# Four array tiles for the second token half of the chunk products, gates behind the last pair, a merged Nyquist product and a later norm, in an fp32 three-layer kernel

## The chip, the cores and the metric

One core of one Trainium2 chip. The metric is the device time of one execution in microseconds (us), as the median of three runs. The profile is that of one execution of its own, taken by the hardware profiler.

## What is computed

The input is 512 tokens of 1024 features, in fp32. A first block (feed-forward, token mixer, feed-forward, norm), an "even" layer (Fourier mixing beside attention) and an "odd" layer (gated linear recurrence) with a last norm follow each other. What the change touches of it:

```python
def first_block(x, ...):
    x = x + 0.5 * swiglu(rms_norm(x, ffn1_norm), ...)
    x = x + token_mixer(rms_norm(x, mix_norm), ...)
    x = x + 0.5 * swiglu(rms_norm(x, ffn2_norm), ...)
    return rms_norm(x, final_norm)

# token_mixer: p = h @ w_in; a gated convolution (y_a), and per head of 64
def step(S, inp):                      # wkv7, 512 tokens one after the other
    r_t, w_t, k_t, v_t, a_t, b_t = inp
    sa = einsum("bhvk,bhk->bhv", S, a_t)
    S = S * w_t + sa[..., None] * b_t + v_t[..., None] * k_t
    return S, einsum("bhvk,bhk->bhv", S, r_t)
y_b = (groupnorm(y) + bonus) * g @ w_out_b
return (sigmoid(g_a) * y_a + sigmoid(g_b) * y_b) @ w_o

# even layer: h = rms_norm_2(x, norm_g), f_in = 4 groups of 256 features
fmix = fftn(fg, axes=(1, 3), norm="ortho").real
fmix = einsum('bsgc,gce->bsge', fmix, fourier_w)
```

## The kernel before

Activations lie feature-major as tiles of 128 features by 512 tokens. TensorE has a fast fp32 form (fp32r) that keeps only a part of the digits, so every large product is written as three (`mm3`): a tile is split into a high half and the rest (`split`: `h`/`l`, weights `wh`/`wl`, scaled inputs `xh`/`xl`), and h·h, h·l and l·h are added up in PSUM. Such a matmul is `128*128 128x512 f32` in the rows. Weights come in groups of 128x1024 (`group`): `raw` is loaded, `wh` is cast from it on ACT or DVE, and `wl` is formed on DVE or, for many later weights, was written to DRAM during the first feed-forward (`low`) and is loaded again.

Nothing is issued where it is written. Class `Rec` records every operation; `schedule` then plays the program on a cost model (`_cost`, with buffers and PSUM banks counted) and picks the next instruction of each engine, mostly by its place in the program plus `rec.bias`; `choose` prefers, within limits, a matmul of the array mode in use. `emit` fixes the order that comes out. So the place of a call in the code is a priority, and a price in `_cost` can move work. All operations carry one line, L555 (L557 in the changed kernel).

The stages on the time axis: first feed-forward to about 400 us, mixer to about 740, second feed-forward to about 1140, even layer to about 1475, odd layer and last norm to the end.

In the mixer the 512 steps of the recurrence are done in 8 chunks of 64 tokens, for two heads at a time (a "pair", four of them). `pair(j)` makes the scaled keys, queries and so on; `pair_out(j)` does the chunks: `batch` forms their products, `inverse64` inverts 64x64 triangular matrices from 16x16 inverses in two levels (`p1 = b·TT`, copied to `x1`; `p2 = x1·T`, added to `T`), `pd = T·R` and `pq = ak·R` apply the inverse, `pm` makes the chunk's transition, and a chain over the chunks follows. These products are plain fp32 with operands of 64 partitions, and TensorE then works as four tiles of 64x64 (row half by column half). A product whose operand lies in partitions 0 to 63 uses the upper row half, and where it writes in PSUM says which column half. In `p1`, `p2`, `pd` and `pq` the chunk of half `c` is read from half `c` and written to half `c`, so that two of the four tiles work:

```python
            p1 = self.W((128, 8, 64))
            for m in range(8):
                for c in range(2):
                    k = slice(64 * c, 64 * c + 64)
                    PE.matmul(p1[k, m], b[k, m], TT[k, m], start=True, stop=True)
```

The other chunk products (`xy`, `pm`) use all four. The products of 64x64 stand in the rows as `64*64 64x64` or, with 128 columns, `64*64 64x128`; one such fp32 product leaves two records in the trace. `W` and `P` take one of 8 PSUM banks.

Around the chunk work, `conv`, `out_a`, `gate` and `gates` do the rest of the mixer with large matmuls. At its end, the last pair's `yc` is transposed, `yo` is formed from it on DVE and POOL, split into `h` and `l`, and used by `w_out_b`; the results `gt` go through POOL and a split into `w_o`.

In `_even`, two sums of squares of x (`sumsq`: squares on ACT, additions on DVE for the first and on POOL for the second) are folded over the partitions by matmuls with a matrix of ones (`fold`, in the rows `h,rones` and `l,rones`), and give `rs1` and `rs`; matmuls of the Fourier weights `e_f` start on the unnormed `xs` meanwhile. Then, for each of four groups, a first DFT (`d1h`, `d1l`), sums and differences `s`, `d` over the token halves, and three products over the other axis (`seq`), the third for one column only, the Nyquist one: `pn = seq(c2, 0)`, 12 matmuls of 256 columns, of which row 0 is used.

Of the kernel before, what the change touches and what calls it, by code (L numbers as in the profile page):

```python
# [71 lines left out]
_COFF["mI"] = _COFF["i64"] + 64  # L72
_COFF["mST"] = _COFF["mI"] + 64
_COFF["m16"] = _COFF["mST"] + 64
_COFF["e16"] = _COFF["m16"] + 64
_COFF["eps"] = _COFF["e16"] + 128
_COFF["reset"] = _COFF["eps"] + 4
_NC = _COFF["reset"] + 512
# [2 lines left out]
def _const_block():  # L81
    c = np.zeros((128, _NC), np.float64)
    p = np.arange(128)[:, None]
    q = np.arange(128)[None, :]
    same = (p // 64) == (q // 64)
    m = {
        "ident": p == q,
        "ones": np.ones((128, 128)),
        "bones": same,
    }  # L90
    for n in _CST:
        c[:, _COFF[n]:_COFF[n] + 128] = m[n]
# [4 lines left out]
    c[:, _COFF["m16"]:_COFF["m16"] + 64] = (w // 32 == p % 64 // 32) & (w % 32 < 16) & (p % 32 >= 16)  # L97
    c[:, _COFF["e16"]:_COFF["e16"] + 128] = np.repeat(np.eye(16).reshape(2, 128), 64, 0)
# [499 lines left out]
def _cost(o, outs, ins):  # L598
# [4 lines left out]
    if o.eng == "tensor":  # L603
        if o.fn == "matmul":
            m = _elems(ins[0])
            k = int(ins[0].shape[0])
            up = lambda i: 32 if i <= 32 else 64 if i <= 64 else 128
            o.mode = up(k), up(m)
            one = "float32r" in str(ins[0].dtype)
            c = n / 2.4 + 13.5 if one else max(n, m) / 0.6 + 10.0  # L610
            o.load = n / (2.4 if one else 0.6) * o.mode[0] * o.mode[1] / 16384.0
            if not one and m <= 64 and k <= 64:
                c = 31.0 if n <= 64 else 105.0
        else:
            o.mode = 128, 128
            c = 109.0
            o.load = 50.0
        return c, 0.0
# [29 lines left out]
class Net:  # L648
# [278 lines left out]
    def _mixer(self):  # L927
# [82 lines left out]
        conv(1)  # L1010
        conv(2)
        self.pair_out(*p.pop(0))
        conv(3)
        p[3] = pair(3)
        out_a(0)
        self.pair_out(*p.pop(1))
        out_a(1)
        out_a(2)
        self.pair_out(*p.pop(2))
        out_a(3)  # L1020
        gates(0, 4)
        self.pair_out(*p.pop(3))
        gates(4, 8)
        ms = []
        for h in range(4):
            w = self.group("w_out_b", h)
# [214 lines left out]
    def inverse64(self, ab, TT):  # L1241

        nc = self.nc
        V, A, PE = nc.vector, nc.scalar, nc.tensor
        f = lambda t: t.rearrange("p m i -> p (m i)")
        a16 = self.T(shape=(128, 8, 64), p="a16")
        nc.tt(a16, ab, self.c("m16", 64).unsqueeze(1).to_broadcast([128, 8, 64]), ALU.mult)
        for lvl in range(2):

            b = ab if lvl else a16  # L1250
            T = self.T(shape=(128, 8, 64), p="TN")
            V.transpose(out=f(T), in_=f(TT))
            p1 = self.W((128, 8, 64))
            for m in range(8):
                for c in range(2):
                    k = slice(64 * c, 64 * c + 64)
                    PE.matmul(p1[k, m], b[k, m], TT[k, m], start=True, stop=True)
            x1 = self.T(shape=(128, 8, 64), p="XT")
            A.copy(x1, p1)
            p2 = self.W((128, 8, 64))  # L1260
            for m in range(8):
                for c in range(2):
                    k = slice(64 * c, 64 * c + 64)
                    PE.matmul(p2[k, m], x1[k, m], T[k, m], start=True, stop=True)
            if lvl:
                for h in (0, 64):
                    V.tensor_tensor(T[h + 32:h + 64, :, 0:32], T[h + 32:h + 64, :, 0:32], p2[h + 32:h + 64, :, 0:32], ALU.add)
            else:
                V.tensor_tensor(T, T, p2, ALU.add)
                TT = self.T(shape=(128, 8, 64), p="TT")  # L1270
                V.transpose(out=f(TT), in_=f(T))
        return T

    def batch(self, AR, BK, BH, dF, vT, ab, TT):
# [10 lines left out]
        for tp in range(2):  # L1285

            xy = [self.W((128, 6, 64)) for _ in range(2)]
            for tt in range(2):
                for i in range(2):
                    for hh, cc in q4:  # L1290
                        PE.matmul(xy[hh][sl(cc), 2 * i + tt], BK[tp][sl(hh), tt, i, sl(cc)], AR[tp][sl(hh), tt, 1, sl(cc)],
                                  start=True, stop=True)
                for hh, cc in q4:
                    PE.matmul(xy[hh][sl(cc), 4 + tt], AR[tp][sl(hh), tt, 0, sl(cc)], BK[tp][sl(hh), tt, 1, sl(cc)],
                              start=True, stop=True)
            t = self.T(p="ak")[:, 0:256].rearrange("p (q s) -> p q s", q=4)
            for hh in range(2):
                V.tensor_tensor(RR[tp][hh].rearrange("p i t s -> p (i t) s")[:, :, 0:64], xy[hh][:, 0:4], mI, ALU.mult)
                V.tensor_tensor(t[:, 2 * hh:2 * hh + 2], xy[hh][:, 4:6], mST, ALU.mult)
            ak.append(t)  # L1300

        for tp in range(2):
# [8 lines left out]
            A.copy(t[:, 0], pa)  # L1311
# [4 lines left out]
        for tp in range(2):  # L1316
            pd = self.W((128, 4, 128))
            for hh in range(2):
                for tt in range(2):
                    q = 2 * hh + tt  # L1320
                    for cc in range(2):
                        PE.matmul(pd[sl(cc), q], T[sl(cc), 4 * tp + q], RR[tp][hh][sl(cc), 0, tt], start=True, stop=True)
            for hh in range(2):
                A.copy(RR[tp][hh][:, 0], pd[:, 2 * hh:2 * hh + 2])
        for tp in range(2):
            pq = self.W((128, 4, 128))
            for hh in range(2):
                for tt in range(2):
                    q = 2 * hh + tt
                    for cc in range(2):  # L1330
                        PE.matmul(pq[sl(cc), q], ak[tp][sl(cc), q], RR[tp][hh][sl(cc), 0, tt], start=True, stop=True)
            for hh in range(2):
                V.tensor_tensor(RR[tp][hh][:, 1], RR[tp][hh][:, 1], pq[:, 2 * hh:2 * hh + 2], ALU.add)
# [4 lines left out]
        for tp in range(2):  # L1338
# [3 lines left out]
            for tt in range(2):  # L1342
                for hh, cc in q4:
                    R = RR[tp][hh]
                    PE.matmul(pm[cc][sl(hh), tt, 0:128], aT[tp][sl(cc), 0, tt, sl(hh)], R[sl(cc), 0, tt], start=True, stop=True)
                for hh, cc in q4:
                    R = RR[tp][hh]
                    PE.matmul(pm[cc][sl(hh), tt, 128:192], R[sl(cc), 1, tt, 64:128], vT[sl(cc), 2 * tp + tt, sl(hh)],
                              start=True, stop=True)
            Rh = aT[tp][:, 1]  # L1350
            for cc in range(2):
                V.tensor_tensor(cc4(MT)[:, cc], pm[cc][:, :, 64:128], dv[:, cc, 2 * tp:2 * tp + 2], ALU.add)
                A.copy(cc4(N)[:, cc], pm[cc][:, :, 128:192])
# [9 lines left out]
    def _even(self):  # L1363
# [37 lines left out]
        for gp in range(2):  # L1401
# [10 lines left out]
        fo = []  # L1412
        for g in range(4):
            fs = []
            for m in range(2):
# [18 lines left out]
            V.tensor_tensor(s, pp[0], b, ALU.add)  # L1434
            V.tensor_tensor(d, pp[0], b, ALU.subtract)
            sd = (self.split(s, (128, 2, 256)), self.split(d, (128, 2, 256)))

            def seq(col, tr):
                ps = self.P((128, 2, 256))
                for e in range(2):  # L1440
                    h, l = sd[e]
# [410 lines left out]
```

## Time and profile before

| | |
|---|---|
| median of three runs | 1857.87 us (1857.47 to 1860.03) |
| the profiled execution's own time | 1858.05 us |
| its span, first to last instruction | 1856.3 us |
| TensorE busy | 1835.8 us, 99% |
| VectorE (DVE) busy | 1266.8 us, 68% |
| ScalarE (ACT) busy | 854.5 us, 46% |
| GpSimd (POOL) busy | 230.5 us, 12% |
| mean granted clock of TensorE | 0.997 of full |

The profiled execution lies 0.18 us above the median. The span and 1.75 us around it make its time.

### The profile page before, as it was taken

What the parts mean: (1) busy time and instruction counts of PE and PEld (TensorE: products, weight loads), DVE (VectorE), ACT (ScalarE), POOL (GpSimd) and SP (SyncE); (2) the same over time, 40 slices, a digit from 0 to 9 for tenths busy, and PEclk for the clock granted to TensorE, in tenths of its full rate; (3) what the DMA queues carried; (4) which work ended last, traced back from release to release, by engine and by line L of the source; (5) the groups of instructions that cost most, each with busy time, mean ns of one, the idle gap of its engine ahead of it and who ended that gap; (6) DMA issues with size and microseconds to landing.
All of it is one profiled execution on the core that took longest, in us unless ns stands there. A gap on an engine that the chain in (4) does not pass through costs nothing.

```text
span 1856.3 us, 26407 instructions
## 1 busy us (share of the span) xinstructions
PE 1835.8 (99%) x10344; PEld 1540.4 (83%) x10344; DVE 1266.8 (68%) x1966; ACT 854.5 (46%) x1188; POOL 230.5 (12%) x182
## 2 busy tenths in 40 slices
PE   9999999999999999999999999999999999999997
PEld 7888888888888886888878887888999888888887
DVE  7766775579767424476567668854478966899773
ACT  6333433465243332344344246422255645897771
POOL 0100101223202003211011015110000010000002
PEclk9999999999999999999999999999999999999999
DMA  7898895436534344578888874222212125466543
GB/s 270 285 311 283 299 318 173 142 128 172 189 120 139 131 154 157 176 260 291 271 273 306 283 239 146 81 69 79 89 50 72 54 102 188 169 204 210 193 170 103
DMA packets 120398, 341.10 MB, mean 184 GB/s; under 512 B 33873, under 2 KB 36177, under 8 KB 120273
## 3 DMA queue, kind: packets, MB, share of 16 engines
q1 hardware_dynamic: 120272, 339.41, 54.6%
q8 instruction: 81, 1.33, 0.3%
q14 instruction: 45, 0.36, 0.1%
HBM read 277.76 MB, written 61.60 MB: 183 GB/s over the span
## 4 chain that ended last, share of the span: by engine, by line
PE 53%; DMA 6%; DVE 5%; ACT 1%; issue 1%; POOL 1%; SPq 0%; POOLq 0%; DVEq 0%; ACTq 0%
PE pm L555 51%; DMA raw<-o_in 3%; PE pw L555 2%; DVE wl L555 2%; DMA low<-wl 2%; ACT wh L555 1%; DMA raw<-ffn_d 1%; DVE t L555 0%; DVE l L555 0%; DMA wl<-low 0%; POOL acc L555 0%; DVE x L555 0%; DVE xl L555 0%; DVE acc L555 0%; DVE s L555 0%
## 5 line engine op out<-in xcount | busy, mean ns | idle before, releaser
L555 ACT CAST wh<-raw 128x1024 fp32r<-128x1024 f32 (+1 forms) x331 | 343.8, 1042 | 670.6 <-PE pm L555 285.2
L555 PE MATMUL pm<-xh,wl 128*128 128x512 f32 x1488 | 580.6, 390 | 1.3 <-DVE wl L555 1.1
L555 PE MATMUL pm<-xh,wh 128*128 128x512 f32 x1488 | 581.3, 391 | 0.3 <-ACT wh L555 0.3
L555 PE MATMUL pm<-xl,wh 128*128 128x512 f32 x1488 | 580.6, 390 | 0.9 <-DVE xl L555 0.9
L555 DVE TENSOR_TENSOR wl<-raw,wh 128x1024 fp32r<-128x1024 f32 (+1 forms) x302 | 383.1, 1271 | 194.9 <-DMA low<-wl 86.7
L555 PEld LDWEIGHTS pm<-xh,wl 128*128 128x128 f32 x1488 | 279.4, 188 | 60.9 <-DVE wl L555 3.9
L555 PEld LDWEIGHTS pm<-xh,wh 128*128 128x128 f32 x1488 | 279.4, 188 | 58.7 <-ACT wh L555 0.7
L555 PEld LDWEIGHTS pm<-xl,wh 128*128 128x128 f32 x1488 | 279.4, 188 | 58.6 <-DVE xl L555 1.3
L555 PE MATMUL pm<-h,wl 128*128 128x512 f32 (+1 forms) x832 | 317.8, 382 | 2.1 <-DMA wl<-low 2.1
L555 PE MATMUL pm<-h,wh 128*128 128x512 f32 (+1 forms) x832 | 316.8, 383 | 1.8 <-DVE yo L555 0.9
L555 PE MATMUL pm<-l,wh 128*128 128x512 f32 (+1 forms) x832 | 317.5, 382 | 0.0
L555 POOL TENSOR_TENSOR t<-t,t 128x512 f32<-128x512 f32 x60 | 90.3, 1507 | 915.3 <-DVE t L555 693.7
L555 PEld LDWEIGHTS pm<-h,wl 128*128 128x128 f32 x832 | 156.8, 189 | 32.3 <-DMA wl<-low 2.6
L555 PEld LDWEIGHTS pm<-h,wh 128*128 128x128 f32 x832 | 156.8, 189 | 32.4 <-DVE h L555 1.3
L555 PEld LDWEIGHTS pm<-l,wh 128*128 128x128 f32 x832 | 156.9, 189 | 30.1 <-DVE l L555 0.2
L555 DVE TENSOR_TENSOR t<-pm,rstd 128x512 f32<-128x512 f32 x146 | 98.8, 684 | 15.4 <-PE pm L555 15.3
L555 ACT ACT_TABLE_LOAD x72 | 92.4, 1283 | 17.2 <-DVE s L555 15.5
L555 DVE CAST wh<-raw 128x1024 fp32r<-128x1024 f32 x77 | 56.6, 735 | 63.9 <-PE pm L555 38.8
L555 DVE TENSOR_TENSOR x<-x,pm 128x512 f32<-128x512 f32 (+1 forms) x44 | 27.8, 637 | 68.7 <-PE pm L555 68.6
L555 ACT ACTIVATE t<-t 128x512 f32<-128x512 f32 x100 | 59.4, 625 | 26.7 <-DVE t L555 25.7
L555 POOL TENSOR_TENSOR acc<-acc,sq 128x512 f32<-128x512 f32 x28 | 46.7, 1667 | 151.1 <-ACT sq L555 151.1
L555 DVE TENSOR_TENSOR l<-t,h 128x512 fp32r<-128x512 f32 x87 | 59.7, 695 | 6.8 <-ACT h L555 5.7
(257 smaller groups left out, 2052.9 us busy)
## 6 DMA issues: line engine op xcount, KB each, us to landing
low<-wl SPq DMA_DIRECT2D x106, 512.0 KB, 3.7
wl<-low SPq DMA_DIRECT2D x106, 512.0 KB, 3.5
raw<-w_in SPq DMA_DIRECT2D x76, 512.0 KB, 4.7
raw<-o_in SPq DMA_DIRECT2D x64, 512.0 KB, 4.6
raw<-ffn_g SPq DMA_DIRECT2D x44, 512.0 KB, 4.2
raw<-ffn_u SPq DMA_DIRECT2D x44, 512.0 KB, 4.9
raw<-ffn_d SPq DMA_DIRECT2D x32, 512.0 KB, 4.9
raw<-o_out SPq DMA_DIRECT2D x32, 512.0 KB, 4.7
```

The costliest lines, as they stand in the source:

```text
L555: o.ins = getattr(getattr(self.nc, o.eng), o.fn)(*o.args, **o.kw)
```

## The change

1. `inverse64`, `batch`: for the second token half (`tp` = 1) the products write to the other half of the PSUM partitions (`c ^ tp`), so that, with the first half's products between them, all four tiles are used. `p1`, `p2`, `pd` and `pq` become two PSUM tiles each, one for a token half. What is needed on the other half is copied there by ACT: `Ts` (two copies of 64x256 for each level), `aT` of `tp` = 1 in two copies instead of one, `x1` in two copies of 128x256 instead of one of 128x512. A mask `m32` (64 more columns of the constant block) and a second masked tile let the level-2 addition cover the whole tile. `pd` and `pq` run over `hh` outside and `tp` inside.
2. The mixer's order: `pair(3)` before `conv(3)`, `pair_out(1)` before `out_a(0)`, and all eight gates behind the last `pair_out` (four stood ahead of it).
3. `_even`: `rec.bias = 100` for the two sums of squares and what follows them.
4. `_even`: the Nyquist columns of the four groups are gathered in two tiles `nyq` (two memsets, 16 copies of 128x2) and multiplied once: 12 matmuls of 128x256 instead of 48. For that the loop over the groups is cut in two; all first DFTs come first.
5. `_cost`: the planner's price of a 64x128 fp32 product goes from 105 to 62 ns.

```diff
-                c = 31.0 if n <= 64 else 105.0
+                c = 31.0 if n <= 64 else 62.0
...
-        conv(3)
         p[3] = pair(3)
+        conv(3)
+        self.pair_out(*p.pop(1))
         out_a(0)
-        self.pair_out(*p.pop(1))
...
-        gates(0, 4)
         self.pair_out(*p.pop(3))
-        gates(4, 8)
+        gates(0, 8)
...
+            Ts = self.T(p="Ts")[:, 0:256].rearrange("p (m i) -> p m i", m=4)
+            for c in range(2):
+                A.copy(Ts[64 - 64 * c:128 - 64 * c], T[64 * c:64 * c + 64, 4:8])
+            p1 = [self.W((128, 4, 64)) for _ in range(2)]
+            for m in range(4):
+                for tp in range(2):
+                    for c in range(2):
+                        k, o = slice(64 * c, 64 * c + 64), 64 * (c ^ tp)
+                        PE.matmul(p1[tp][o:o + 64, m], b[k, 4 * tp + m], TT[k, 4 * tp + m], start=True, stop=True)
             x1 = self.T(shape=(128, 8, 64), p="XT")
+            for tp in range(2):
+                A.copy(x1[:, 4 * tp:4 * tp + 4], p1[tp])
...
+        pd = [self.W((128, 4, 128)) for _ in range(2)]
+        for hh in range(2):
+            for tt in range(2):
+                q = 2 * hh + tt
+                for tp in range(2):
                     for cc in range(2):
+                        PE.matmul(pd[tp][sl(cc ^ tp), q], T[sl(cc), 4 * tp + q], RR[tp][hh][sl(cc), 0, tt], start=True, stop=True)
+            for tp in range(2):
+                A.copy(RR[tp][hh][:, 0], pd[tp][:, 2 * hh:2 * hh + 2])
...
+        self.rec.bias = 100
         s1 = self.sumsq(adds="vector")
...
+        self.rec.bias = 0
...
+        ps = self.P((128, 2, 256))
+        for e in range(2):
+            for k in range(2):
+                self.mm3(ps[:, e], nyq[0][:, e, k], nyq[1][:, e, k], d2h[0][e][:, k], d2l[0][e][:, k], k == 0, k == 1)
+        pn = self.T(shape=(128, 2, 256), p="pn")
+        A.copy(pn, ps)
...
-            pn = seq(c2, 0)
-            V.tensor_copy(Q[0:1], pn[0:1])
+            V.tensor_copy(Q[0:1], pn[32 * g:32 * g + 1])
```

What the planner makes of it is seen in the order of instructions. The first place is TensorE in the first pair's `inverse64`, where the second level's `p2` is formed (`TN` is T, `XT` is x1, `Ts` the copy of T on the other half). Before:

```order
L555 MATMUL pm_1000<-xl_687,wh_1003 128x512
L555 MATMUL pm_1000<-xh_686,wl_1002 128x512
L555 MATMUL pw_964<-TN_961,XT_963 64x64 x16
L555 MATMUL pm_1000<-xh_688,wh_1003 128x512
L555 MATMUL pm_1000<-xl_689,wh_1003 128x512
```

The same place in the changed kernel:

```order
L557 MATMUL pm_1007<-xh_688,wh_1010 128x512
L557 MATMUL pw_970<-TN_965,XT_969 64x64 x2
L557 MATMUL pw_971<-Ts_966,XT_969 64x64 x2
L557 MATMUL pw_970<-TN_965,XT_969 64x64 x2
L557 MATMUL pw_971<-Ts_966,XT_969 64x64 x2
L557 MATMUL pw_970<-TN_965,XT_969 64x64 x2
L557 MATMUL pw_971<-Ts_966,XT_969 64x64 x2
L557 MATMUL pw_970<-TN_965,XT_969 64x64 x2
L557 MATMUL pw_971<-Ts_966,XT_969 64x64 x2
L557 MATMUL pm_1007<-xl_689,wh_1010 128x512
```

It is still one run of 16 products between large matmuls, but the products of the two token halves alternate, two by two, and go to two PSUM tiles. Over the whole program the stretches of 64x64 work between large matmuls go from 32 to 44.

The second place is TensorE at the end of the mixer, where the last pair's `yc` is transposed and the split of `yo` (h_1317, in the changed kernel h_1325) is used first. Before:

```order
L555 MATMUL pw_1315<-cst,yc_1310 128x128 x4
L555 MATMUL pm_1372<-h_992,wh_1368 128x512
L555 MATMUL pm_1372<-l_993,wh_1368 128x512
L555 MATMUL pm_1372<-h_992,wl_1367 128x512
L555 MATMUL pm_1372<-h_1132,wh_1368 128x512
L555 MATMUL pm_1372<-l_1133,wh_1368 128x512
L555 MATMUL pm_1372<-h_1132,wl_1367 128x512
L555 MATMUL pm_1372<-h_1222,wh_1368 128x512
L555 MATMUL pm_1372<-l_1223,wh_1368 128x512
L555 MATMUL pm_1372<-h_1222,wl_1367 128x512
L555 MATMUL pm_1342<-h_1317,wh_1341 128x512
L555 MATMUL pm_1345<-h_1317,wh_1341 128x512
```

The changed kernel there, with the middle of it left out (15 more matmuls):

```order
L557 MATMUL pw_1323<-cst,yc_1318 128x128 x4
L557 MATMUL pm_1382<-h_1243,wl_1377 128x512
L557 MATMUL pm_1388<-h_999,wh_1387 128x512
L557 MATMUL pm_1388<-l_1000,wh_1387 128x512
...
L557 MATMUL pm_1391<-l_1244,wh_1387 128x512
L557 MATMUL pm_1391<-h_1243,wl_1386 128x512
L557 MATMUL pm_1397<-h_999,wh_1396 128x512
L557 MATMUL pm_1370<-h_1325,wh_1369 128x512
L557 MATMUL pm_1373<-h_1325,wh_1369 128x512
```

Nine matmuls stood between the transposes and the first use of `h`; now 20 do. From that first use to the first matmul of `w_o` there were 24 and are 41, and the low half of `w_o`'s second group, issued 26 matmuls ahead of its use before, is issued 40 ahead.

The third place is ACT in the even layer's norm, where the two sums (acc_2045 and acc_2058 before, acc_2073 and acc_2086 now; the second of each is added up on POOL) are split for `fold`. Before:

```order
L555 CAST wh_2130<-raw_2129 128x1024
L555 CAST h_2225<-t_2093 128x512
L555 CAST h_2054<-acc_2045 128x512
L555 CAST h_2067<-acc_2058 128x512
L555 CAST wh_2138<-raw_2137 128x1024
```

In the changed kernel:

```order
L557 ACTIVATE sq_2093<-x_1410,vec 128x512
L557 CAST h_2095<-acc_2086 128x512
L557 CAST wh_2171<-raw_2170 128x1024
L557 CAST h_2082<-acc_2073 128x512
L557 ACT_TABLE_LOAD
```

POOL's sum now comes first on ACT, and DVE's stands behind it and a weight cast. On TensorE the first `h,rones`, which is that of DVE's sum, stands 33 matmuls behind the last one of the second feed-forward.

## Rows read from the trace of the kernel before

**Rows 1.** The page, busy time of the engines.
```profile
PE 1835.8 (99%) x10344; PEld 1540.4 (83%) x10344; DVE 1266.8 (68%) x1966; ACT 854.5 (46%) x1188; POOL 230.5 (12%) x182
```

**Rows 2.** Waits of TensorE by releaser: us in total, times, longest.
```profile
PE pm L555 <- ACT h L555: 2.2, 1, 2.2
PE pm L555 <- DMA wl<-low: 2.1, 1, 2.1
```

**Rows 3.** Timeline of TensorE, 64-column runs: start, length, count, idle before.
```profile
416.02 0.39 PE L555 MATMUL pm<-l,h 128*128 128x512 f32 x1
416.34 0.69 PE L555 MATMUL pw<-bk,ar 64*64 64x64 f32 x32
416.96 0.50 PE L555 MATMUL pm<-h,l 128*128 128x512 f32 x1
...
443.85 0.39 PE L555 MATMUL pm<-xh,wl 128*128 128x512 f32 x1
444.17 0.69 PE L555 MATMUL pw<-bk,ar 64*64 64x64 f32 x32
...
446.20 0.50 PE L555 MATMUL pm<-h,rbones 128*128 128x512 f32 x1
...
501.23 0.39 PE L555 MATMUL pm<-xh,wh 128*128 128x512 f32 x1
501.55 1.15 PE L555 MATMUL pw<-TT,ab 64*64 64x64 f32 x32
502.63 0.50 PE L555 MATMUL pm<-xl,wh 128*128 128x512 f32 x1
```

**Rows 4.** Timeline of TensorE, runs of 128 columns.
```profile
569.11 1.93 PE L555 MATMUL pw<-R,TN 64*64 64x128 f32 x32
570.86 1.82 PE L555 MATMUL pw<-R,ak 64*64 64x128 f32 x30
...
572.57 0.70 PE L555 MATMUL pw<-R,aT 64*64 64x128 f32 x14
573.04 0.33 PE L555 MATMUL pw<-vT,R 64*64 64x64 f32 x6
```

**Rows 5.** Timelines of TensorE and SyncE's queue, end of the mixer.
```profile
720.74 0.63 PE L555 MATMUL pw<-cst,yc 128*128 128x128 f32 x4
...
725.46 1.20 PE L555 MATMUL pm<-h,wh 128*128 128x512 f32 x4 [0.85 <-DVE h L555]
...
735.89 0.77 PE L555 MATMUL pm<-h,wl 128*128 128x512 f32 x1 [2.15 <-DMA wl<-low]
...
739.42 0.40 PE L555 MATMUL pm<-l,wh 128*128 128x512 f32 x1
...
728.88 0.38 SPq L555 DMA_DIRECT2D wl<-low  x1
```

**Rows 6.** Windows: length, busy time of each engine, granted clock, DMA share, GB/s.
```profile
735.00:740.00 5.00, 4.11 (x11) 3.27 (x12) 3.77 (x4) 2.98 (x5) 5.00 (x4) 0.66 1.02 410
```

**Rows 7.** Timelines of TensorE, POOL and ACT, even layer's norm.
```profile
1139.41 0.39 PE L555 MATMUL pm<-l,wh 128*128 128x512 f32 x1
1139.64 0.39 PE L555 MATMUL pm<-h,wl 128*128 128x512 f32 x1
...
1142.82 1.28 POOL L555 TENSOR_TENSOR acc<-acc,sq 128x512 f32<-128x512 f32 x1
1144.33 5.38 POOL L555 TENSOR_TENSOR acc<-acc,sq 128x512 f32<-128x512 f32 x1 [0.23 <-ACT sq L555]
...
1150.27 2.00 ACT L555 CAST wh<-raw 128x1024 fp32r<-128x1024 f32 x2
...
1150.41 0.50 PE L555 MATMUL pm<-h,rones 128*128 128x512 f32 x1 [2.19 <-ACT h L555]
```

**Rows 8.** Timeline of TensorE, matmuls of 128x256 in the Fourier part.
```profile
1220.50 0.28 PE L555 MATMUL pm<-h,l 128*128 128x256 f32 x1
1220.62 0.40 PE L555 MATMUL pm<-xh,wh 128*128 128x512 f32 x1
```

More of the change, by code (lines that the diff above doesn't have):

```diff
@@ L74 @@
 _COFF["m16"] = _COFF["mST"] + 64
-_COFF["e16"] = _COFF["m16"] + 64
+_COFF["m32"] = _COFF["m16"] + 64
+_COFF["e16"] = _COFF["m32"] + 64
 _COFF["eps"] = _COFF["e16"] + 128
@@ L97, in _const_block @@
     c[:, _COFF["m16"]:_COFF["m16"] + 64] = (w // 32 == p % 64 // 32) & (w % 32 < 16) & (p % 32 >= 16)
+    c[:, _COFF["m32"]:_COFF["m32"] + 64] = (w < 32) & (p % 64 >= 32)
     c[:, _COFF["e16"]:_COFF["e16"] + 128] = np.repeat(np.eye(16).reshape(2, 128), 64, 0)
@@ L1012, in _mixer @@
         self.pair_out(*p.pop(0))
+        p[3] = pair(3)
         conv(3)
-        p[3] = pair(3)
+        self.pair_out(*p.pop(1))
         out_a(0)
-        self.pair_out(*p.pop(1))
         out_a(1)
@@ L1245, in inverse64 @@
         f = lambda t: t.rearrange("p m i -> p (m i)")
-        a16 = self.T(shape=(128, 8, 64), p="a16")
-        nc.tt(a16, ab, self.c("m16", 64).unsqueeze(1).to_broadcast([128, 8, 64]), ALU.mult)
+        bs = []
+        for m in ("m16", "m32"):
+            t = self.T(shape=(128, 8, 64), p="a16")
+            nc.tt(t, ab, self.c(m, 64).unsqueeze(1).to_broadcast([128, 8, 64]), ALU.mult)
+            bs.append(t)
         for lvl in range(2):
-            b = ab if lvl else a16
+            b = bs[lvl]
@@ L1251, in inverse64 @@
             T = self.T(shape=(128, 8, 64), p="TN")
             V.transpose(out=f(T), in_=f(TT))
[L1253 to L1257, printed above, removed]
-            x1 = self.T(shape=(128, 8, 64), p="XT")
[L1259 to L1269, printed above, removed]
+            Ts = self.T(p="Ts")[:, 0:256].rearrange("p (m i) -> p m i", m=4)
+            for c in range(2):
+                A.copy(Ts[64 - 64 * c:128 - 64 * c], T[64 * c:64 * c + 64, 4:8])
+            p1 = [self.W((128, 4, 64)) for _ in range(2)]
@@ new lines, in inverse64 @@
+            for m in range(4):
[3 more added lines that the diff above has]
+                        PE.matmul(p1[tp][o:o + 64, m], b[k, 4 * tp + m], TT[k, 4 * tp + m], start=True, stop=True)
+            x1 = self.T(shape=(128, 8, 64), p="XT")
+            for tp in range(2):
+                A.copy(x1[:, 4 * tp:4 * tp + 4], p1[tp])
+            p2 = [self.W((128, 4, 64)) for _ in range(2)]
@@ L1270, in inverse64 @@
+            for m in range(4):
+                for tp in range(2):
+                    for c in range(2):
+                        o, k = 64 * c, slice(64 * (c ^ tp), 64 * (c ^ tp) + 64)
+                        PE.matmul(p2[tp][o:o + 64, m], x1[k, 4 * tp + m], Ts[k, m] if tp else T[k, m], start=True, stop=True)
+            for tp in range(2):
+                Tt = T[:, 4 * tp:4 * tp + 4]
+                V.tensor_tensor(Tt, Tt, p2[tp], ALU.add)
+            if not lvl:
                 TT = self.T(shape=(128, 8, 64), p="TT")
@@ L1293, in batch @@
                 for hh, cc in q4:
-                    PE.matmul(xy[hh][sl(cc), 4 + tt], AR[tp][sl(hh), tt, 0, sl(cc)], BK[tp][sl(hh), tt, 1, sl(cc)],
+                    PE.matmul(xy[hh][sl(cc ^ tp), 4 + tt], AR[tp][sl(hh), tt, 0, sl(cc)], BK[tp][sl(hh), tt, 1, sl(cc)],
                               start=True, stop=True)
@@ L1310, in batch @@
             t = self.T(shape=(128, 2, 2, 128), p="aT")
-            A.copy(t[:, 0], pa)
+            if tp:
+                for c in range(2):
+                    A.copy(t[sl(1 - c), 0], pa[sl(c)])
+            else:
+                A.copy(t[:, 0], pa)
             aT.append(t)
@@ L1315, in batch @@
         T = self.inverse64(ab, TT)
[L1316 to L1320, printed above, removed]
-                    for cc in range(2):
[L1322 to L1329, printed above, removed]
+        pd = [self.W((128, 4, 128)) for _ in range(2)]
+        for hh in range(2):
+            for tt in range(2):
+                q = 2 * hh + tt
+                for tp in range(2):
+                    for cc in range(2):
+                        PE.matmul(pd[tp][sl(cc ^ tp), q], T[sl(cc), 4 * tp + q], RR[tp][hh][sl(cc), 0, tt], start=True, stop=True)
+            for tp in range(2):
+                A.copy(RR[tp][hh][:, 0], pd[tp][:, 2 * hh:2 * hh + 2])
+        pq = [self.W((128, 4, 128)) for _ in range(2)]
+        for hh in range(2):
+            for tt in range(2):
+                q = 2 * hh + tt
+                for tp in range(2):
                     for cc in range(2):
-                        PE.matmul(pq[sl(cc), q], ak[tp][sl(cc), q], RR[tp][hh][sl(cc), 0, tt], start=True, stop=True)
-            for hh in range(2):
-                V.tensor_tensor(RR[tp][hh][:, 1], RR[tp][hh][:, 1], pq[:, 2 * hh:2 * hh + 2], ALU.add)
+                        k = sl(cc ^ tp)
+                        PE.matmul(pq[tp][sl(cc), q], ak[tp][k, q], RR[tp][hh][k, 0, tt], start=True, stop=True)
+            for tp in range(2):
+                V.tensor_tensor(RR[tp][hh][:, 1], RR[tp][hh][:, 1], pq[tp][:, 2 * hh:2 * hh + 2], ALU.add)
         ch = lambda t: t.rearrange("p t (c i) -> p c t i", c=2)
@@ L1344, in batch @@
                     R = RR[tp][hh]
-                    PE.matmul(pm[cc][sl(hh), tt, 0:128], aT[tp][sl(cc), 0, tt, sl(hh)], R[sl(cc), 0, tt], start=True, stop=True)
+                    k = sl(cc ^ tp)
+                    PE.matmul(pm[cc][sl(hh), tt, 0:128], aT[tp][k, 0, tt, sl(hh)], R[k, 0, tt], start=True, stop=True)
                 for hh, cc in q4:
                     R = RR[tp][hh]
-                    PE.matmul(pm[cc][sl(hh), tt, 128:192], R[sl(cc), 1, tt, 64:128], vT[sl(cc), 2 * tp + tt, sl(hh)],
+                    PE.matmul(pm[cc ^ tp][sl(hh), tt, 128:192], R[sl(cc), 1, tt, 64:128], vT[sl(cc), 2 * tp + tt, sl(hh)],
                               start=True, stop=True)
@@ L1352, in batch @@
                 V.tensor_tensor(cc4(MT)[:, cc], pm[cc][:, :, 64:128], dv[:, cc, 2 * tp:2 * tp + 2], ALU.add)
-                A.copy(cc4(N)[:, cc], pm[cc][:, :, 128:192])
+                A.copy(cc4(N)[:, cc], pm[cc ^ tp][:, :, 128:192])
             for cc in range(2):
@@ L1411, in _even @@
             fw.append((p, m))
-        fo = []
+        nyq = [self.T(F32R, (128, 2, 2, 128), "ny") for _ in range(2)]
+        for t in nyq:
+            G.memset(t.bitcast(F32), 0.0)
+        sds = []
         for g in range(4):
@@ L1436, in _even @@
             sd = (self.split(s, (128, 2, 256)), self.split(d, (128, 2, 256)))
+            for e in range(2):
+                for t, hl in zip(nyq, sd[e]):
+                    nc.copy(t[:, e, :, 32 * g:32 * g + 1], hl[:, :, 128:129])
+            sds.append(sd)
+        ps = self.P((128, 2, 256))
+        for e in range(2):
+            for k in range(2):
+                self.mm3(ps[:, e], nyq[0][:, e, k], nyq[1][:, e, k], d2h[0][e][:, k], d2l[0][e][:, k], k == 0, k == 1)
+        pn = self.T(shape=(128, 2, 256), p="pn")
+        A.copy(pn, ps)
+        fo = []
+        for g in range(4):
             def seq(col, tr):
@@ L1440, in seq @@
                 for e in range(2):
-                    h, l = sd[e]
+                    h, l = sds[g][e]
                     for k in range(2):
```

## The prediction, made before the changed kernel ran

> **What bounds the kernel now.** I read the page first: TensorE is busy for 99% of the span [rows 1], while DVE, ACT and POOL have large idle shares in the table. So time comes out of this kernel in two ways only: fewer or cheaper TensorE instructions, or the closing of one of its few gaps. The list of its waits comes next: the two longest are 2.2 us behind ACT's `h` and 2.1 us behind a load of a low half [rows 2]. Then the timeline of TensorE, for what an instruction costs from its start to the next start (lengths overlap and say less). The reader is to see that one 128x512 matmul follows the other after 0.23 us [rows 7], one of 128x256 after 0.12 [rows 8], and that no run of 64x64 products has idle time in front of it [rows 3, 4].
>
> **Chunk products.** First the price of today's kinds. A four-tile run of 32 records stands between 416.02 and 416.96, one of 128 records between 443.85 and 446.20 [rows 3]. Less one matmul of 0.23 they take 0.71 and 2.12; the difference of 96 records gives 14.7 ns a record, and 0.71 - 32 x 0.0147 = 0.24 us are left for the change of array mode. The matmul behind each run is 0.11 longer than usual (0.50 against 0.39), so a run costs 0.35 us beside its records. The two-tile run at 501.55 takes 502.63 - 501.23 - 0.23 = 1.17, less 0.24 that is 29.1 ns a record. A product is two records: 58.1 ns on two tiles, 29.4 on four. With 128 columns the start-to-start times are 1.75 us for 32 records (R,TN, two tiles) and 0.47 for 14 (R,aT, four) [rows 4]: 109.4 and 67.1 ns a product.
>
> By the loops each pair has 64 products of 64 columns in `p1` and `p2` (two levels, two steps, 16 each) and 32 of 128 columns in `pd` and `pq`. If all go from two tiles to four: 4 x 64 x 28.7 ns = 7.4 us, and 4 x 32 x 42.3 ns = 5.4; together **-12.8**. Below this stands nothing, if the new products overlap no better than today's; above it nothing either, as four tiles are all there are.
>
> What speaks for the full gain is that a tile's own pace is the same today in both kinds: 2 x 58 = 116 ns a product on two tiles, 4 x 29.4 = 118 on four. The two-tile products write both row halves' results into one PSUM bank, the four-tile ones put the row halves into two banks; sharing a bank has cost nothing. The new products share a bank as the two-tile ones do, but from all four tiles at a time, and no row shows that. The Trainium skill, "TensorEngine Tiling (Array Packing)", Restrictions and Gotchas, says that different row tiles cannot access the same PSUM bank at one time. By that rule the gain would be near nothing and the whole sum near -3; the trace's equal pace of a tile speaks against it, so I give it a small chance as a rival.
>
> The planner cuts this work into 44 runs where it had 32. Twelve more changes of mode at 0.35 are **+4.2**. I keep 0.35 and not the 0.24, as the longer matmul behind a run comes each time.
>
> The copies that the change adds (`Ts`, the second `aT` and `x1`) are ACT's, which is idle for half of the span. What they can cost is a wait of TensorE between two steps of one pair, since a step now needs a copy that it didn't need. Today none of the runs waits [rows 3, 4], because the planner puts large matmuls between; in the new order it still does. I take **+1.2**: half a dozen waits of 0.2, between 0 and 8 (0.18 for each of 44 runs).
>
> **End of the mixer.** From the transposes at 720.74 to the matmul at 739.42 [rows 5] the order has 52 matmuls. At 0.23 they take 11.96, and four transposes 0.44 (720.74 with a pace of 0.11): 12.4, where 18.68 passed. So 6.3 us are lost there: a wait for a PSUM bank, 0.85 for DVE's `h`, 2.15 for a low half [rows 5], and then 8 matmuls in 3.53 us instead of 1.84: the granted clock was 0.66 in this stretch [rows 6], between its two levels of 2.4 and 1.2 GHz, after TensorE had stood three times within 15 us. From the transposes to `h` the chain over DVE and POOL takes 725.46 - 720.74 = 4.72. With 20 matmuls in between (4.60, and 0.44 for the transposes) TensorE arrives at 5.04: 0.3 us of slack. The low half that was late had been issued at 728.88 and released TensorE at 735.89, 7.0 us later, its use 26 matmuls (6.0 us) behind the issue. It is now 40 (9.2 us) behind, and no other transfer is moved ahead of it. The four gates that move cost nothing themselves: they are the same matmuls, and the gate tiles `gt` are needed only behind `w_out_b`. I take the whole gain, rounded: **-6.2**, between -2.3 (the low half late again, with its 3.9 of wait and clock) and -6.3.
>
> **Nyquist.** 36 fewer matmuls of 0.12 us [rows 8]: **-4.3**. Two memsets on POOL and 16 tiny copies cost TensorE nothing unless it stands for them. Two chains get shorter cover: the last copies into `nyq` before the merged product, and `pn` before the first group's `Q`. By my count of the matmuls between, each has 2.3 to 2.7 us for a chain of about that length. **+0.8** for both, between 0 and 1.8 (two waits like the 0.85 at 725.46 [rows 5]).
>
> **The norm.** From the last matmul of the feed-forward at 1139.64 to the first use of POOL's sum at 1150.41 [rows 7] 29 matmuls are issued, 6.67 us; 10.77 passed, so 4.1 are lost today. The cause is POOL: its last addition took 5.38 us, where the one before took 1.28, and the split and the fold wait for it. With the bias this work comes later on all engines, but DVE's sum, which TensorE needs first, is split on ACT behind POOL's sum and a weight cast. TensorE is there 34 x 0.23 = 7.8 us behind the last feed-forward matmul. If POOL ends as late as today (1149.71, 10.1 us behind it), then 0.6 of split, 1.0 of cast and another 0.6 follow: 12.4, a stall of 4.6. If POOL needs 1.3, there is none. The same DVE additions and casts run beside POOL in the new order, so I take 4.0. A gap of 2.15 at the end of the mixer brought the low clock and cost 1.7 (3.53 - 1.84); one of 2.19 here did not. For a gap of 4 I take 1.2 of that. 5.2 against the 4.1 of today: **+1.1**, between -4.1 and +2.2.
>
> Parts at nothing: the wider constant block (64 columns more of 1348, loaded while the first feed-forward runs), the second mask (DVE or POOL, both far from full), the new price in `_cost` (it acts only through the order that has been counted). The second feed-forward and everything from the first `e_out` on keep their order, and with it their small waits.
>
> **Sum.** -12.8 + 4.2 + 1.2 - 6.2 - 4.3 + 0.8 + 1.1 = -16.0. Against the profiled execution's 1858.05 that is 1842.05; the median lies 0.2 lower: **1842**.
>
> **Rivals.**
> - *Tiles of two row halves do not overlap in one bank.* The 12.8 go: 1854.8. For it: no row with four tiles on one bank. Against it: the equal pace per tile. 6%.
> - *The other side: the chunk work becomes a chain of copies.* Each of the 44 runs starts with a wait, since the two token halves now go through TensorE together, and no half is left to cover the other's copy from PSUM. The mechanism decides when a run waits for more than 0.36 us (16.0 / 44, with the 1.2 already in); at 0.6 the time is 1842 - 1.2 + 26.4 = 1867. Against it: the planner has large matmuls to put between, and none of today's 32 runs waits. The Trainium skill, "TensorEngine Tiling (Array Packing)", Performance Considerations, warns that after tiling the copies out of PSUM can become the bottleneck; here ACT's half-idle share speaks against it. 4%.
> - *The fold waits longer.* ACT's order makes DVE's sum wait for POOL's, which ends later than today because its additions are all later: stall 7 and the full 1.7 of the clock, 8.7 instead of 5.2: 1845.5. For it: the order on ACT. 20%.
> - *Norm and copies are hidden altogether.* POOL's additions at 1.3, no waits in chunk work and Fourier part: 5.2 + 1.2 + 0.8 less, 1834.8. 14%.
> - *The low half of `w_o` is late again.* Its loads start when buffers come free, not by the count of matmuls: 3.9 more, 1845.9. 12%.
>
> **Numbers.** The forecast has 44%. Two per thousand, 3.7 us, is about what a measurement tells from no change here. The forecast, the long fold, the hidden norm and the late low half are all faster by more: 0.90. The shared bank gives 3.1 less than before, which is the same: 0.06; the chain of copies is slower: 0.04. The range goes from the hidden norm, 1834, to the two late cases together with some of the 8 us of waits at the runs, 1851, and leaves out the shared bank and the chain of copies.
>
> **What the profile of the changed kernel would show.** Runs of `TN,XT` and `Ts,XT` at 15 ns a record, and of `R,TN` at 34: right; at 29 and 55 the tiles do not overlap. About 44 runs without idle time ahead of them. No wait at the transposes of the last `yc`, at its `h` and at the first `w_o`, and a full clock there. A wait of about 4 us for ACT's `h` at the even layer's first fold. 12 matmuls with `ny`. What would make it wrong above all are waits inside the chunk work, which no row of before has, and POOL's additions in the norm, whose length depends on what runs beside them.

## The result and the profile after

| | before | changed |
|---|---|---|
| median | 1857.67 us (1855.56 to 1860.03, four runs) | 1841.49 us (1840.80 to 1842.02, four runs) |
| profiled execution, span | 1858.05, 1856.3 | 1842.02, 1840.2 |

The ratio is 0.9915 (95% interval 0.990 to 0.993): faster by 16 us, as the sum had it. The sum came out, but not all of its terms. The page of the changed kernel, its span and the engines:

```profile
span 1840.2 us, 26413 instructions
PE 1823.0 (99%) x10308; PEld 1523.8 (83%) x10308; DVE 1269.4 (69%) x1970; ACT 866.3 (47%) x1231; POOL 240.1 (13%) x189
```

TensorE is busy 12.8 us less and still for 99% of the time [rows 1]; 36 records are gone. Its waits, by releaser (total, times, longest):

```profile
PE pm L557 <- ACT h L557: 2.2, 2, 1.3
...
PE pm L557 <- DVE R L557: 1.3, 1, 1.3
PE pm L557 <- DVE xl L557: 0.9, 2, 0.6
PE pm L557 <- DVE l L557: 0.8, 2, 0.6
PE pw L557 <- DVE t L557: 0.7, 1, 0.7
```

The waits for `wl<-low` and for one `h` of 2.2 [rows 2] are gone, and there are more short ones. TensorE's timeline of two runs that went from two tiles to four (start, length, count):

```profile
503.37 0.39 PE L557 MATMUL pm<-xh,wl 128*128 128x512 f32 x1
503.69 0.69 PE L557 MATMUL pw<-TT,a 64*64 64x64 f32 x32
504.32 0.50 PE L557 MATMUL pm<-xh,wh 128*128 128x512 f32 x1
...
512.65 0.67 PE L557 MATMUL pw<-R,TN 64*64 64x128 f32 x16
513.14 0.41 PE L557 MATMUL pw<-ar,bk 64*64 64x64 f32 x16
```

Read as the prediction did: 504.32 - 503.37 - 0.23 = 0.72 us for the same 32 records that took 1.17 [rows 3], less 0.24 that is 15.0 ns a record; and 0.49 / 16 = 30.6 ns for R,TN, which took 54.7 [rows 4]. Four tiles overlap on shared banks as they do on separate ones.

At the end of the mixer (timeline of TensorE, then windows, columns as in [rows 6]):

```profile
711.96 0.60 PE L557 MATMUL pw<-cst,yc 128*128 128x128 f32 x4
712.31 0.48 PE L557 MATMUL pm<-h,wl 128*128 128x512 f32 x1
...
716.75 1.08 PE L557 MATMUL pm<-h,wh 128*128 128x512 f32 x4
```
```profile
715.00:720.00 5.00, 5.00 (x24) 4.11 (x23) 2.79 (x5) 1.30 (x2) 2.10 (x2) 1.00 0.04 7
720.00:725.00 5.00, 5.00 (x24) 4.14 (x23) 4.98 (x8) 3.41 (x5) 5.00 (x4) 1.00 0.95 291
725.00:730.00 5.00, 5.00 (x24) 4.14 (x23) 4.71 (x5) 2.81 (x4) 5.00 (x4) 1.00 1.06 404
```

TensorE is busy without a gap at the full granted clock. The DMA share rises late here too (0.04, then 0.95 and more), so the loads of `w_o` did not come earlier against the transposes (the first low half is issued 6.8 us behind them here and 6.9 before); TensorE has more to do meanwhile.

To see where the 16 us lie, I cut both timelines at the same matmuls and took from each stretch what its matmuls need at 0.227 us (128x512), 0.12 (128x256) and 0.109 (transposes):

| stretch | before | changed | difference | predicted |
|---|---|---|---|---|
| start to the first chunk product | 416.34 | 418.52 | +2.2 | 0 |
| mixer, of it: | 334.21 | 323.33 | -10.9 | -13.6 |
| inside the runs of 64x64 work, waits taken out | 57.54 | 48.57 | -9.0 | -11.0 |
| entering and leaving them (32 and 44 runs) | 6.38 | 8.69 | +2.3 | +2.4 |
| waits inside the runs | 0.00 | 0.69 | +0.7 | |
| other losses, stalls at the end with them | 9.15 | 4.24 | -4.9 | -5.0 (waits +1.2, end -6.2) |
| lost in the second feed-forward | 1.78 | 0.06 | -1.7 | 0 |
| lost from its last matmul to the transposes of `rs` | 4.30 | 2.45 | -1.9 | +1.1 |
| Fourier part to the odd layer's first fold | | | -3.9 | -3.5 |
| the rest | | | +0.1 | 0 |

In the column of the prediction its 0.35 us a run is divided as its rows have it: 0.09 in front of a run and 0.11 behind it are entering and leaving, and 0.15 lies inside.

### The profile page after: what moved, and what is told of

It is laid out like the page before. It is cut to its first block, busy times and chain, and to the rows that moved or that the text cites. A ratio compares the mean times of both kernels' runs of the same rounds, so it can differ in the third digit from the quotient of the medians.

```text
span 1840.2 us, 26413 instructions
## 1 busy us (share of the span) xinstructions
PE 1823.0 (99%) x10308; PEld 1523.8 (83%) x10308; DVE 1269.4 (69%) x1970; ACT 866.3 (47%) x1231; POOL 240.1 (13%) x189
## 3 DMA queue, kind: packets, MB, share of 16 engines
q1 hardware_dynamic: 120272, 339.44, 54.7%
## 4 chain that ended last, share of the span: by engine, by line
PE 87%; DVE 5%; DMA 4%; issue 1%; ACT 1%; SPq 0%; POOL 0%; POOLq 0%; ACTq 0%; DVEq 0%
PE pm L557 83%; PE pw L557 4%; DMA raw<-w_in 2%; DVE wl L557 1%; DVE t L557 1%; DVE u L557 1%; ACT wh L557 1%; DMA raw<-ffn_g 0%; DMA n<-dab 0%; DMA raw<-ffn_d 0%; DVE acc L557 0%; SPq L557 0%; DMA x<-xT 0%; DMA raw<-ffn_u 0%; DVE xl L557 0%
```

## The experiments

Each kernel was timed beside the kernel before on the same chip; the runs of e1 to e4 shared one set, and so did e5 to e8 and e9 to e11. Ranges are those of all runs. The kernel before had medians of 1857.51, 1858.73 and 1857.50 in the three sets, and 1857.67 beside the changed kernel, so a difference between kernels of different sets is good to about 1 us.

**e1, the same order on two tiles.** Every `c ^ tp` becomes `c`, and the copies stay without their move:

```diff
-                A.copy(Ts[64 - 64 * c:128 - 64 * c], T[64 * c:64 * c + 64, 4:8])
+                A.copy(Ts[64 * c:64 * c + 64], T[64 * c:64 * c + 64, 4:8])
...
-                        k, o = slice(64 * c, 64 * c + 64), 64 * (c ^ tp)
+                        k, o = slice(64 * c, 64 * c + 64), 64 * c
```

> The changed kernel with every product of the second token half written to the same half of the PSUM partitions as the first's, so that two of the four tiles work again; the order on every engine, the split PSUM tiles, the copies (now without a move between halves), the later norm and the merged Nyquist product all stay. Theory 1 (the gain in the chunk products is the overlap of the tiles): 512 records of 64 columns at 29.1 instead of 14.7 ns and 256 of 128 columns at 54.7 instead of 33.6 come back, 12.8 us, so about 1854 us. Rival (the gain came from the order and from two half-sized PSUM tiles, tiles overlap little more than before): 1841 to 1845 us.

Measured 1852.03 us (1850.30 to 1854.62), 0.997 of before (0.9959 to 0.9981), so 10.5 above the changed kernel. The run of `TT,a` from above, in this kernel:

```profile
502.87 0.39 PE L557 MATMUL pm<-xh,wl 128*128 128x512 f32 x1
503.19 1.15 PE L557 MATMUL pw<-TT,a 64*64 64x64 f32 x32
504.27 0.50 PE L557 MATMUL pm<-xh,wh 128*128 128x512 f32 x1
```

1.17 us where four tiles take 0.72. Summed over the 44 runs, waits taken out, 60.46 us against 48.57: the tiles' overlap is worth 11.9. With the 32 runs of before it was 57.54 for the same records: 12 more runs cost 2.9 inside and 2.3 at their borders, 0.43 each. Theory 1 holds. The time moves by 10.5 and not by 11.9; that the slower products arrive later at the mixer's waits, which are 1.5 us shorter in this trace, would account for it.

**e2 to e4, three parts alone.** e2 is the changed kernel with the mixer's order, the norm and the Nyquist product of before. e3 is the kernel before with this edit, e4 with part 4 of the change and nothing else:

```diff
-        conv(3)
         p[3] = pair(3)
+        conv(3)
+        self.pair_out(*p.pop(1))
         out_a(0)
-        self.pair_out(*p.pop(1))
...
-        gates(0, 4)
         self.pair_out(*p.pop(3))
-        gates(4, 8)
+        gates(0, 8)
```

> The kernel before with only the four-tile products and the planner's price. Theory 1: in its runs it saves the 9 us that the changed kernel's trace shows (57.5 to 49.3 less a wait of 0.7 inside), pays about 2 for entering and leaving more runs and up to 2 at the start, and keeps the 6.3 us of stalls at the end of the mixer: 1851 to 1853 us. Rival (new waits between the steps of a pair eat the gain when the order of the mixer is not changed with it): 1856 us or more.

> The kernel before with only the mixer's new order (third pair and second pair_out earlier, all gates behind the last pair_out). Theory 1: the stalls at the end of the mixer, 6.3 us, go, and one or two of the new waits (0.9 to 1.5 each) come: 1852 to 1854 us. Rival (the stalls went because the four-tile products end earlier, and stay here): 1857 to 1858 us.

> The kernel before with only the Nyquist columns of the four groups multiplied at once. Nothing in front of the Fourier part moves. Theory 1: 36 matmuls of 0.12 us less and about 0.4 us of new losses: 1853.5 to 1854 us. Rival (16 tiny copies and the wait for the last group delay the chain of the first groups): 1856 us or more.

Measured: e2 1853.43 us (1851.57 to 1857.32), ratio 0.9978 (0.9969 to 0.9987); e3 1854.23 (1852.33 to 1857.34), 0.9981 (0.9972 to 0.9990); e4 1854.21 (1851.59 to 1858.32), 0.9982 (0.9973 to 0.9992); before 1857.51. Each lies 0.2 to 0.4 us above the range of theory 1 and 1.8 or more below that of its rival, so theory 1 holds in all three. In e2's trace the waits at the end of the mixer are there, 6.5 us of them where before has 3.9; in e3's they are gone, but 1.9 us of waits stand inside the 64x64 runs, where the changed kernel has 0.7. The three parts give 10.7 together and the whole change 16. The norm is part of the difference (e5). The remaining 2 to 4 us would be what order and tiles gain only together, as these two traces suggest; the intervals of the three times leave some 3 us open, so it isn't settled. e3's profile is that of its slowest execution. The new price in the planner (part 5) and the two other moves of part 2 have no run of their own.

e4 also tells how firm the stalls of before were, since up to the Fourier part it is that kernel:

```profile
735.28 0.50 PE L555 MATMUL pm<-h,wl 128*128 128x512 f32 x1 [1.21 <-DMA wl<-low]
735.61 0.40 PE L555 MATMUL pm<-h,wh 128*128 128x512 f32 x1
```
```profile
735.00:740.00 5.00, 4.72 (x21) 3.92 (x22) 4.26 (x5) 2.50 (x5) 5.00 (x4) 1.00 1.01 410
```

The low half is late by 1.21 and not 2.15 [rows 5], the clock stays at 1.00 and not 0.66 [rows 6], and the same mixer takes 331.60 us instead of 334.21.

**e5, without the later norm; e6, with the gates in two halves.**

```diff
-        self.rec.bias = 100
...
-        self.rec.bias = 0
```
```diff
         out_a(3)
+        gates(0, 4)
         self.pair_out(*p.pop(3))
-        gates(0, 8)
+        gates(4, 8)
```

> The changed kernel with the even layer's two sums of squares at their old place (no bias). Nothing in front of the norm moves. Theory 1 (the later norm is worth what it took off the fold's wait): the stretch from the last feed-forward matmul to the transposes of rs loses 4.3 us again (6.4 where the clock falls) instead of 2.4: 1843 to 1845 us. Rival (the wait depends on whether POOL or DVE gets through, not on the bias): 1841 to 1842 us.

> The changed kernel with four gates ahead of the last pair_out again and four behind it; the rest of the new order stays. Theory 1 (the eight gates behind the last pair are what covers its chain): stalls at the last yc and h come back, 4 to 6 us: 1845 to 1848 us. Rival (the cover comes from the earlier third pair and second pair_out): 1841 to 1843 us.

e5: 1843.22 us (1842.13 to 1845.04), 0.9921 (0.9908 to 0.9935). The stretch of the norm loses 5.8 us, and its longest wait is that of before (timelines of POOL and TensorE):

```profile
1132.18 5.21 POOL L557 TENSOR_TENSOR acc<-acc,sq 128x512 f32<-128x512 f32 x1 [0.33 <-ACT sq L557]
...
1138.10 0.50 PE L557 MATMUL pm<-h,rones 128*128 128x512 f32 x1 [2.12 <-ACT h L557]
```

The bias is worth 1.4 to 1.7 by the medians (against the result and against e9 below), 1.1 to 1.9 by the ratios and 3.0 to 3.4 by this stretch; 1.4 of its 5.8 is a lower clock behind the wait, which the kernel before's trace (4.3) doesn't have. The ranges of e5 and e9 overlap, so the trace carries this verdict more than the time. e6: 1849.21 us (1848.50 to 1850.04), 0.9952 (0.9939 to 0.9966), 7.7 more than the changed kernel (6.9 by the ratios) and 1.2 above the range of theory 1. TensorE's timeline there:

```profile
717.53 0.47 PE L557 MATMUL pm<-h,wh 128*128 128x512 f32 x1 [1.60 <-DVE yc L557]
...
721.82 0.63 PE L557 MATMUL pw<-cst,yc 128*128 128x128 f32 x4 [1.97 <-DVE yc L557]
723.35 0.79 PE L557 MATMUL pm<-h,wh 128*128 128x512 f32 x1 [0.90 <-DVE yo L557]
723.94 0.63 PE L557 MATMUL pm<-l,wh 128*128 128x512 f32 x1
724.37 0.63 PE L557 MATMUL pm<-h,wl 128*128 128x512 f32 x1
```

The four gates are what covers the last pair's chain; with them ahead of it the faster products only arrive earlier at its waits, and behind the last of these three the matmuls follow at 0.43 us instead of 0.23, as they did behind 735.89 in [rows 5].

**e7, a still later norm; e8, the same with fewer runs.** e7 sets the bias to 140. e8 also lets the planner stay longer in an array mode:

```diff
-        self.near, self.wait = 400, 3000.0
+        self.near, self.wait = 600, 3000.0
```

> The changed kernel with a bias of 140 instead of 100 on the norm: 49 matmuls instead of 34 stand between the last one of the feed-forward and the first fold, and rs is transposed 14 matmuls later. Theory 1 (the fold waits for DVE's sum, which was late by 1.3 us): the wait goes, 1.3 to 2.4 us less, 1839 to 1840 us. Rival (the backlog on DVE is moved along and the products with rs wait instead): 1841 to 1843 us.

> As the one before, and the planner may prefer a matmul of the array mode in use up to 600 places away, where it was 400: 40 stretches of 64x64 work instead of 44. Theory 1 (each change into 64x64 work and back costs 0.43 us: 5.2 us for 12 between the kernel before and the two-tile kernel): 1.7 us less than the one before, 1837.5 to 1838.5 us. Rival (what is saved in changes comes back as waits, because the pairs' steps end later): as the one before or slower.

e7: 1844.86 us (1844.29 to 1845.19), 0.9928 (0.9916 to 0.9941): slower than the changed kernel, and than both forecasts. e8: 1844.09 us (1842.98 to 1846.35), also 0.9928. In e7 the wait moved to another place, that of the last `xl`; timelines of TensorE, DVE and POOL, and the window:

```profile
1136.52 0.79 PE L557 MATMUL pm<-xl,wh 128*128 128x512 f32 x1 [2.69 <-DVE xl L557]
...
1132.48 2.32 DVE L557 TENSOR_TENSOR wl<-raw,wh 128x1024 fp32r<-128x1024 f32 x1
1134.72 1.75 DVE L557 SCALAR_TENSOR_TENSOR xl<-x,g,xh 128x512 fp32r<-128x512 f32 x1
...
1131.85 1.86 POOL L557 TENSOR_TENSOR acc<-acc,sq 128x512 f32<-128x512 f32 x1 [1.09 <-ACT sq L557]
1134.55 1.37 POOL L557 TENSOR_TENSOR acc<-acc,sq 128x512 f32<-128x512 f32 x1 [0.83 <-ACT sq L557]
```
```profile
1135.00:1140.00 5.00, 3.48 (x8) 2.81 (x9) 5.00 (x7) 1.67 (x2) 0.92 (x1) 0.58 0.46 131
```

`wl` takes 2.32 and `xl` 1.75 beside POOL's additions, where `xl` needs 0.73 alone; the granted clock falls to 0.58. e8 has the same wait (2.5) and its mixer takes 325.15 us instead of 323.33: four runs fewer, but 1.7 us of waits at the runs instead of 0.7, and 1.5 for one `h` instead of 0.9. That is the rival's mechanism, in a profile of e8's slowest execution. The times don't decide: e8's median is 0.8 below e7's, where theory 1 had 1.7 and the rival none, and the ranges overlap.

That gave a second theory of the norm, that its wait comes from DVE and POOL slowing each other. In the changed kernel the rows are these (timelines of TensorE, DVE, POOL):

```profile
1139.26 0.50 PE L557 MATMUL pm<-h,rones 128*128 128x512 f32 x1 [1.26 <-ACT h L557]
...
1135.64 2.31 DVE L557 TENSOR_TENSOR wl<-raw,wh 128x1024 fp32r<-128x1024 f32 x1
1137.88 0.68 DVE L557 TENSOR_TENSOR acc<-acc,sq 128x512 f32<-128x512 f32 x1
...
1135.30 1.57 POOL L557 TENSOR_TENSOR acc<-acc,sq 128x512 f32<-128x512 f32 x1 [1.40 <-ACT sq L557]
```

POOL ended early, at 1136.87. What came last was DVE's own addition, behind a `wl` of 2.31. TensorE waits 1.26 to 1.30 us here in all four executions with this norm (e1, e6 and e9 beside this one).

**e9 to e11, the changed kernel again, and with both sums on DVE.** e10 has a bias of 60, e11 of 100:

```diff
-        self.rec.bias = 100
+        self.rec.bias = 60
...
-        s2 = self.sumsq(lambda k: self.v("final_norm", k))
+        s2 = self.sumsq(lambda k: self.v("final_norm", k), adds="vector")
```

> The changed kernel once more, as a measure beside the next two and for how much its stretches vary from run to run. The mixer's waits of 0.9, 0.7 and 1.3 us (rbones, aT, the bank behind R) come again at the same places if they belong to the order; the losses at the start (0.65) and in the second feed-forward (0.1 to 2.4 so far) move if they belong to the loads. 1841 to 1842 us.

> The changed kernel with both sums of squares of the even norm added up on DVE and a bias of 60; POOL does none of it. Theory 2 (the norm's wait comes from DVE and POOL slowing each other: wl took 2.31 beside POOL's addition and 1.21 without, POOL's addition 5.21 beside DVE and 1.29 without): without POOL's part each takes its short time, seven more additions of 0.67 on DVE notwithstanding; the wait at the fold is under 1 us and the stretch loses 1 to 2 us instead of 2.4: 1840 to 1841.5 us. Rival (DVE's own backlog is the cause, so 4.7 us more work on DVE makes it worse): the stretch loses 4 to 7 us, 1843 to 1846 us.

> As the one before with the bias of 100: the second sum's last additions come behind the first fold, which needs only the first sum. Theory 2: the wait at the fold is smallest here, 1839.5 to 1841 us. Rival: as the one before or worse, 1843 to 1846 us.

e9: 1841.78 us (1839.79 to 1843.06), 0.9911 (0.9894 to 0.9927). e10: 1839.47 (1838.48 to 1841.41), 0.9902 (0.9887 to 0.9917). e11: 1841.00 (1839.06 to 1842.22), 0.9908 (0.9893 to 0.9923). The stretch of the norm loses 2.8, 1.5 and 1.3 us. DVE in e10:

```profile
1130.68 1.22 DVE L557 TENSOR_TENSOR wl<-raw,wh 128x1024 fp32r<-128x1024 f32 x1
1131.82 0.68 DVE L557 TENSOR_TENSOR acc<-acc,sq 128x512 f32<-128x512 f32 x1
1132.42 0.75 DVE L557 SCALAR_TENSOR_TENSOR xl<-x,g,xh 128x512 fp32r<-128x512 f32 x1
1133.08 1.29 DVE L557 TENSOR_TENSOR acc<-acc,sq 128x512 f32<-128x512 f32 x2
```

Each is at its short time again, and the fold has no wait (one of 0.49 for `xl` is left); 4.7 us more work on DVE cost less than sharing with POOL. The traces show theory 2 right; only its forecast that e11 would have the smallest wait at the fold failed (0.52 there, none in e10). e10 has the lowest median of all, 2.3 below the changed kernel of the same set; the ranges overlap, so that it beats the changed kernel is likely and not settled. It beats the kernel before clearly.

## Why the prediction was right, point by point

- **Chunk products, -12.8.** 11.9 by e1. The mechanism and the paces were right. The Trainium skill, "TensorEngine Tiling (Array Packing)", Restrictions and Gotchas, has different row tiles kept from one PSUM bank at one time; here the two row halves write different partitions of one bank at 15.0 ns a record, so as a rule on time it does not hold for them.
- **Twelve more runs, +4.2.** 5.2 by e1 against the kernel before, 0.43 a run and not 0.35. The borders cost 0.19, as the prediction's rows have it (0.09 in front, in its 0.24, and 0.11 behind); what was too small is the part inside a run, 0.24 instead of 0.15.
- **Waits in the chunk work, +1.2.** Too small. The changed kernel has 0.69 inside a run, 0.91 for `h` at 478.40 and 1.29 at 568.40, and the last two come back in every kernel of this order (0.90 to 0.96 and 1.28 in e5, e7 and e9 to e11; e1, with the slower products, has 0.49 and 0.84). With what TensorE needs to start again they are 3.2, against 0.9 of small stalls that left: +2.3. The one at 568.40 is no copy between steps. It waits for a PSUM bank, which DVE frees (timelines of DVE, the first line from another pair, and of POOL):

```profile
501.58 0.27 DVE L557 TENSOR_TENSOR u<-u,n 128x112 f32<-128x112 f32 x1
...
566.06 0.93 DVE L557 TENSOR_TENSOR l<-yo,h 128x512 fp32r<-128x512 f32 x1
566.91 1.11 DVE L557 TENSOR_TENSOR u<-u,n 128x112 f32<-128x112 f32 x1
567.94 0.41 DVE L557 TENSOR_TENSOR R<-R,pw 128x256 f32<-128x256 f32 x1
...
566.40 1.49 POOL L557 TENSOR_TENSOR dF<-cst,s 128x512 f32<-128x512 f32 x1
```

  A step of the next pair's 16x16 inverse stands ahead of the addition that empties `pq`. The prediction looked for new waits on ACT and overlooked DVE's queue. And that step is long only here: it takes 0.26 to 0.28 in the other pairs, with POOL idle, and `l` 0.69 where POOL is idle. So by these rows about 1.1 of the 1.29 is the sharing of DVE and POOL that e10 shows in the norm; no run moves POOL's work away from here.
- **End of the mixer, -6.2.** All stalls left, 6.4 us in these two traces. But e4 shows that the same code loses 2.6 less in another execution, where the clock did not fall, so part of the hit is luck. e6 names the cover: the gates.
- **Nyquist, -4.3 and +0.8.** -3.9, and e4 alone gives 3.3 in the medians. No wait came at either chain; the 0.5 are spread over the stretch.
- **The norm, +1.1.** Wrong in sign: -1.9 in the traces, -1.1 to -1.9 by e5's times. The order on ACT came as forecast; the step that failed is "If POOL ends as late as today", taken because "The same DVE additions and casts run beside POOL in the new order". POOL's last addition took 1.57 and not 5.38 [rows 7], and the fold waited 1.26 for DVE's sum instead of 4.0, because this time DVE paid for the sharing: POOL's addition had started 0.34 ahead of DVE's `wl`, where before (timeline of DVE) it started 0.02 behind one:

```profile
1144.31 1.20 DVE L555 TENSOR_TENSOR wl<-raw,wh 128x1024 fp32r<-128x1024 f32 x1
```

  By its own terms the 12.4 and 4.6 of that paragraph are 12.3 and 4.5.
- **Parts at nothing.** The start lost 2.2 us and the second feed-forward gained 1.7, which no term had. The start shows no effect of the change: among eight profiles with its order (the changed kernel, e1, e5 to e7, e9 to e11) the first chunk product starts between 416.24 and 418.52. In the second feed-forward these eight lose 0.06 to 0.34, and the kernel before, e2, e3, e4 and e8 0.2 to 2.4; a `wl` waits there for an earlier write of a low half, and whether the new order or chance has ended that stays open.

So the sum of -16.0 met 16 by luck as much as by its mechanisms, because its errors cancel: chunk work was 3.0 too hopeful (0.9, 1.0, 1.1), the norm 3.0 too gloomy, and the two stretches with no term nearly cancel. Of the rivals the shared bank fell to e1, and the chain of copies, the long fold and the late low half did not come. The norm was hidden only by the other edit of e10 and e11.

## What to carry to other kernels

Price a packed product by the pace of a tile in runs that the trace already has, and price each entry into the small array mode apart: a run that is cut in two costs 0.4 us here, as much as seven products on two tiles. A faster stage needs its cover moved with it, or it arrives earlier at the same wait (e6). And a wait that is named after one engine may belong to the neighbour that slows it: look at how long the same instruction takes elsewhere in the trace before moving it in the order.

## What the runs showed of the hardware that was not expected

DVE and POOL slow each other, and either may pay: POOL's addition took 5.38 beside DVE and 1.28 without [rows 7], and in e7 DVE's `xl` 1.75 and `wl` 2.32, where e10, without POOL, has 0.75 and 1.22. Over all thirteen traces, none of the 3079 `wl` of 128x1024 that DVE forms with no POOL arithmetic beside them takes more than 1.23; of the 639 with some the longest takes 2.37. The Trainium skill, "GPSIMD Engine Reference", Specifications, says that POOL shares its SBUF interfaces with VectorE and that VectorE's instructions with two SBUF inputs contend with it; all of these have two, so the trace agrees. The clock after a stall differs between executions of one order. At the end of the mixer it was 0.66 after 2.15 us and 1.00 after 1.21. At the even layer's fold, where the waits are nearly equal, 2.19 in the kernel before and 2.12 in e5, whose norm has its order, the 5 us behind them are these (windows, before and e5):

```profile
1150.41:1155.41 5.00, 5.00 (x22) 4.16 (x23) 5.00 (x5) 3.83 (x4) 0.00 (x0) 1.00 0.36 119
1138.10:1143.10 5.00, 5.00 (x15) 3.98 (x16) 4.74 (x5) 3.81 (x4) 0.00 (x0) 0.66 0.46 161
```

The clock was 1.00 in one and 0.66 in the other, with 22 and 15 matmuls, and the stall 4 us ahead was the same too (0.91 and 0.92 for `xl`). So the length of a stall doesn't tell in these runs whether the low clock follows, and what decides it stays open.
